# Attention products of two heads side by side in TensorE's rows, and low parts of weights on GpSimd

## The chip, the cores and the metric

One core of a Trainium2 chip runs the whole program in one launch. The metric is the device time of one execution in microseconds; lower is better. The five engines are TensorE (PE), VectorE (DVE), ScalarE (ACT), GpSimd (POOL) and SyncE (SP, which issues the DMAs). Each works through its own queue in order.

## The reference

Two blocks on a sequence of 256 rows of width 1024, in fp32. The first block runs twice a half feed-forward, a mixer and another half feed-forward. The mixer is attention in three groups (dilations 1, 4, 16) of eight heads of 64, beside a depthwise convolution of 31 taps with a layer norm:

```
q, k, v, glu_in, gates = jnp.split(h @ w_in + b_in, ...)
scores = einsum('..qhd,..khd->..hqk', qblk, kblk) / sqrt(64)   # band masks
p = exp(scores - max);  out = (p @ v) / sum(p);  softmax over the 3 groups
u = a * sigmoid(g);  u = depthwise_conv31(u) + b
y_conv = silu(layernorm(u)) @ w_proj + b_proj
y = (sigmoid(g_attn) * (attn @ w_attn_proj) + sigmoid(g_conv) * y_conv) @ w_out
```

The second block has a mixer of a recurrence and grouped attention (16 query heads, 4 key heads; three branches: compressed keys, selected blocks, window), a convolutional feed-forward, a second mixer without attention and another feed-forward:

```
y_rnn = rg_lru(conv(xr)) * gelu(gr)
o = g0 * softmax(q kc) vc + g1 * softmax(q ks) vs + g2 * softmax(q kw) vw
y = concat([y_rnn, o]) @ w_out
```

## The kernel before

Every large product is split: a weight block of 128x2048 comes from memory as `raw`, ACT casts it to `hi` (L171), DVE or POOL makes `lo = raw - hi` (L175), and three products run for each tile (L191 to L193 with the weight standing in the array, L468 to L470 with the activation standing). `raw`, `hi` and `lo` have three buffers. Where `self.share` is set, POOL makes `lo` in four pieces of 512 columns; else DVE makes it in one.

**The attention of the first block's mixer** (`head`, L656 to L698) takes one head of 64 at a time. Heads 2p and 2p+1 lie in the same tile `QK`, one in rows 0 to 63, one in rows 64 to 127, so a score product has 64 rows of contraction. Per head and half of the queries: three fp32 products into the score bank `sp` (L670), one DVE pass that adds the mask and takes the maximum (L674), exp on ACT (L677), four transposes into the bank `tp` (L680), a copy on ACT (L682), four products with `v` (L685). Each fp32 product is two passes in the trace. After four heads the sum is scaled (L693), transposed and copied (L697, L698). PSUM has one `sp` and one `tp` bank.

**The convolution** runs on DVE beside it (L614, L616). At its end POOL sums two halves (L604, `u`), PE spreads the mean (L709), DVE subtracts (L712), ACT squares (L713), POOL sums over channels (L604, `lns`), PE gives the variance (L724), ACT and PE the row of factors (L736, L738), ACT does Silu (L744), and the cast `cTh` (L492) feeds the last projection (L468).

**The attention of the second block** (`window`, L1320 to L1346, for each of two halves h of the queries, four key heads g, four repeats r) does the same with two score products per window (128 columns each for h=0, 256 for h=1), two DVE passes, two exp, and 2 or 4 transposes and products. `window_out` (L1349) gates the sum; L1377 transposes it. `compressed` and `compressed_out` handle the branch of compressed keys. The GEMM blocks of the same stage fill PE between these steps.

A list scheduler sets the order of each queue ahead of time by priority (the place in the program, shifted by `HEADS` for the first block's heads) and by when it thinks operands are there; `tc.issue_after` adds an order between two instructions and no wait.

Of the kernel before, what the change touches and what calls it, by code (L numbers as in the profile page):

```python
# [10 lines left out]
F32 = mybir.dt.float32  # L11
# [3 lines left out]
AF = mybir.ActivationFunctionType  # L15
OP = mybir.AluOpType
PSUM = bass.MemoryType.PSUM

P = 128
S = 256  # L20
# [24 lines left out]
class Net:  # L45
# [450 lines left out]
    def mixer(self, l, d, xt):  # L496
# [9 lines left out]
        with ExitStack() as es:  # L506
# [148 lines left out]
            def head(h, hd):  # L655
                self.n += 1  # L656
                if hd % 4 == 0:
# [4 lines left out]
                pr, e = hd // 2, slice((hd % 2) * 64, (hd % 2) * 64 + 64)  # L662
                sc = self.spt("sp")

                keys = (((0, 0), (1, 0)), ((h, 1),), ((h, 2),))
                o = 0
                for g in (1, 2, 0) if h else (0, 1, 2):
                    n = P * len(keys[g])
                    ks = slice(keys[g][0][0] * P, keys[g][0][0] * P + n)
                    nc.tensor.matmul(sc[:, o : o + n], QK[e, pr, g, hs], QK[e, pr, 3 + g, ks], start=True, stop=True)  # L670
                    o += n
                sm = wk.tile([P, 512], F32, tag="sg", name=f"sm{self.n}", bufs=2)
                mn = self.small.tile([P, 1], F32, tag="mn", name=f"mn{self.n}")
                dv.tensor_tensor_reduce(  # L674
                    sm, sc, self.mask1[:, h * S : h * S + 512], -0.125, 3.0e38, op0=OP.add, op1=OP.min, accum_out=mn
                )
                nc.scalar.activation(sm, sm, AF.Exp, scale=-1.0, bias=mn, accum_out=den[:, hd % 4 : hd % 4 + 1])  # L677
                pt = self.tpt(True).rearrange("p (k t) -> p k t", t=P)
                for j in range(4):
                    nc.tensor.transpose(pt[:, j], sm[:, j * P : j * P + P], self.ident)  # L680
                pT = wk.tile([P, 4, P], F32, tag="ta", name=f"pT{self.n}", bufs=2)
                nc.scalar.copy(pT, pt)  # L682
                for j, (hh, g) in enumerate(sum((keys[g] for g in ((1, 2, 0) if h else (0, 1, 2))), ())):
                    c0 = g * 512 + hd * 64
                    nc.tensor.matmul(  # L685
                        po[:, hd % 4], pT[:, j], vv[:, hh, c0 : c0 + 64], start=j == 0, stop=j == 3,
                        skip_group_check=True,
                    )
                if hd % 4 == 3:
# [353 lines left out]
    def mixer_ab(self, d, xs, nxt):  # L1043
# [4 lines left out]
        with ExitStack() as es:  # L1048
# [248 lines left out]
            def compressed_out(h, pc, cg):  # L1297
# [6 lines left out]
                for gp in range(2):  # L1304
                    po = self.pot()
# [6 lines left out]


            def window(h, g, r, po, den):
                hs = slice(h * P, h * P + P)
                nk = P * (h + 1)
                gp, e = g // 2, slice((g % 2) * 64, (g % 2) * 64 + 64)
                sc = self.spt("sp")
                for b in range(2):
                    nc.tensor.matmul(  # L1320
                        sc[:, b * nk : b * nk + nk], qr[e, gp * 4 + r, hs], kT[e, b, gp, :nk], start=True, stop=True
                    )
                pe_ = work([512], "pe")
                mn = self.small.tile([P, 2], F32, tag="mn2", name=f"mn2_{self.n}")
                for b in range(2):
                    bs = slice(b * nk, b * nk + nk)
                    dv.tensor_tensor_reduce(
                        pe_[:, bs], sc[:, bs], self.mask2[:, S - nk :], -0.125, 3.0e38,
                        op0=OP.add, op1=OP.min, accum_out=mn[:, b : b + 1],
                    )  # L1330
                    nc.scalar.activation(
                        pe_[:, bs], pe_[:, bs], AF.Exp, scale=-1.0, bias=mn[:, b : b + 1],
                        accum_out=den[:, r, b : b + 1],
                    )
                pt = self.tpt(True)
                for j in range(2 * nk // P):
                    nc.tensor.transpose(pt[:, j * P : j * P + P], pe_[:, j * P : j * P + P], self.ident)
                pT = work([512], "pT")
                nc.scalar.copy(pT[:, : 2 * nk], pt[:, : 2 * nk])
                for b in range(2):  # L1340
                    for kb in range(h + 1):
                        j = b * (h + 1) + kb
                        nc.tensor.matmul(
                            po[:, r, b], pT[:, j * P : j * P + P], vv[:, kb, b, g * 64 : g * 64 + 64],
                            start=kb == 0, stop=kb == h, skip_group_check=True,
                        )  # L1346

# [13 lines left out]
            def attend(h):  # L1361
                hs = slice(h * P, h * P + P)
                c = compressed(h)
                for g in range(4):
                    po = (self.pot() if g % 2 else self.spt("sq")).rearrange("p (r b e) -> p r b e", b=2, r=4)
                    den = self.small.tile([P, 4, 2], F32, tag="den2", name=f"den2_{h}{g}")
# [4 lines left out]
                    window_out(h, g, po, den)  # L1371
                    if g % 2 == 0:
                        continue
                    pt = self.tpt(True)
                    for j in range(4):
                        k = 2 * (g - 1) + j
                        nc.tensor.transpose(pt[:, j * P : j * P + P], ov[:, h, k * P : k * P + P], self.ident)  # L1377
                    ks = slice(2 * (g - 1), 2 * (g - 1) + 4)
# [16 lines left out]

            units = lambda c: [
# [137 lines left out]
```

## Time and profile before

| | |
|---|---|
| median of 3 runs | 2194.73 us (2192.69 to 2194.92) |
| the profiled execution | 2192.24 us, of which 2190.4 are the span |
| busy | PE 97%, DVE 65%, ACT 52%, POOL 25% of the span |
| mean granted TensorE clock | 0.988 |
| first block's attention and convolution | 323.6 to 439.6 and 1021.9 to 1138.0 us |
| its end, to the last projection | 439.6 to 468.5 and 1138.0 to 1166.8 us |
| second block's attention | 1546.4 to 1661 us, its stage to 1688.2 |

The program has five stages without attention, which the change leaves alone. A row of a profile has a time of one execution on the chip; "x6" means six instructions in a row, and a bracket behind it says how long the engine stood idle before it and what ended that.

### The profile page before, as it was taken

The numbers are of one execution on the slowest core, as the hardware profiler recorded it, in microseconds if no ns is written. First come the engines' busy times: TensorE is split into PE (matmuls) and PEld (weight loads), VectorE is DVE, ScalarE is ACT, GpSimd is POOL, SyncE is SP. The second block draws the span as 40 slices with busy tenths as digits, with TensorE's granted clock in tenths as the row PEclk, the third lists the DMA queues.
The fourth block names the chain that finished last, engine by engine and source line by source line (L and its number), as shares of the span: only waits on it lengthen the run. The fifth ranks groups of instructions, "written<-read, shape, count | busy, mean of one in ns | idle before, by whom it ended". The sixth has DMA issues, their size and how long they took to land.

```text
span 2190.4 us, 30888 instructions
## 1 busy us (share of the span) xinstructions
PE 2132.5 (97%) x12158; PEld 1826.5 (83%) x12158; DVE 1430.9 (65%) x2351; ACT 1143.3 (52%) x1582; POOL 537.4 (25%) x431
## 2 busy tenths in 40 slices
PE   8999999999999999999999999899999999999998
PEld 6887988888887788788888888678877998797997
DVE  6844788857876745398866784574555665566664
ACT  5435545565443544555565543584765554546452
POOL 3002985532001100588651200230002000203000
PEclk9999999999999999999999999998999999999999
DMA  9865563447988645455434886554323546554553
GB/s 349 315 203 170 183 192 122 140 135 269 346 294 292 196 155 202 160 191 192 138 103 156 317 290 192 167 143 149 105 77 106 183 154 211 164 186 162 182 175 113
DMA packets 233153, 415.05 MB, mean 189 GB/s; under 512 B 16048, under 2 KB 74288, under 8 KB 233008
## 3 DMA queue, kind: packets, MB, share of 16 engines
q1 hardware_dynamic: 232208, 410.99, 56.2%
q10 hardware_dynamic: 800, 2.10, 0.3%
q8 instruction: 95, 1.56, 0.3%
q14 instruction: 50, 0.41, 0.1%
HBM read 410.94 MB, written 2.11 MB: 189 GB/s over the span
## 4 chain that ended last, share of the span: by engine, by line
PE 87%; DVE 6%; ACT 3%; DMA 2%; issue 1%; POOL 1%; SPq 0%; DVEq 0%; ACTq 0%; POOLq 0%
PE mm L191 18%; PE mm L193 18%; PE mm L192 18%; PE mm L468 8%; PE mm L470 8%; PE mm L469 8%; PE sp L670 2%; PE sp L1320 1%; PE po L685 1%; PE tp L421 1%; PE sp L1192 1%; DMA mraw<-in_mod_w 1%; PE tp L680 1%; DVE lo L175 1%; DMA raw<-in_ffn_w_down 1%
## 5 line engine op out<-in xcount | busy, mean ns | idle before, releaser
L171 ACT CAST hi<-raw 128x2048 fp32r<-128x2048 f32 (+2 forms) x435 | 638.2, 1479 | 526.8 <-PE mm L193 310.5
L175 POOL TENSOR_TENSOR lo<-raw,hi 128x512 fp32r<-128x512 f32 x384 | 501.4, 1340 | 1387.8 <-ACT hi L171 1099.0
L175 DVE TENSOR_TENSOR lo<-raw,hi 128x2048 fp32r<-128x2048 f32 (+1 forms) x249 | 532.6, 2140 | 334.4 <-ACT hi L171 331.6
L191 PE MATMUL mm<-hi,xh 128*128 128x512 f32 (+1 forms) x1200 | 462.3, 386 | 8.3 <-DVE xh L278 5.6
L193 PE MATMUL mm<-hi,xl 128*128 128x512 f32 (+1 forms) x1200 | 460.6, 384 | 2.1 <-DVE xl L270 2.1
L192 PE MATMUL mm<-lo,xh 128*128 128x512 f32 (+1 forms) x1200 | 460.2, 384 | 0.8 <-POOL lo L175 0.6
L468 PE MATMUL mm<-xh,hi 128*128 128x256 f32 x1248 | 355.7, 285 | 0.9 <-ACT gc L756 0.4
L470 PE MATMUL mm<-xh,lo 128*128 128x256 f32 x1248 | 354.8, 284 | 0.0
L469 PE MATMUL mm<-xl,hi 128*128 128x256 f32 x1248 | 354.5, 284 | 0.0
L191 PEld LDWEIGHTS mm<-hi,xh 128*128 128x128 f32 x1200 | 228.1, 190 | 53.7 <-DVE xh L278 8.0
L193 PEld LDWEIGHTS mm<-hi,xl 128*128 128x128 f32 x1200 | 227.6, 190 | 46.5 <-DVE xl L270 3.8
L192 PEld LDWEIGHTS mm<-lo,xh 128*128 128x128 f32 x1200 | 228.0, 190 | 44.2 <-POOL lo L175 2.8
L468 PEld LDWEIGHTS mm<-xh,hi 128*128 128x128 f32 x1248 | 239.0, 192 | 2.7 <-ACT gc L756 0.8
L470 PEld LDWEIGHTS mm<-xh,lo 128*128 128x128 f32 x1248 | 239.0, 191 | 2.5 <-issue 1.3
L469 PEld LDWEIGHTS mm<-xl,hi 128*128 128x128 f32 x1248 | 239.1, 192 | 2.4 <-issue 1.3
L616 DVE SCALAR_TENSOR_TENSOR sp<-u,cols,sp 128x256 f32<-128x256 f32 x464 | 225.4, 486 | 7.8
L191 PE MATMUL mm<-hi,hh 128*128 128x512 f32 x528 | 210.0, 398 | 0.0
L193 PE MATMUL mm<-hi,hl 128*128 128x512 f32 x528 | 209.3, 396 | 0.0
L192 PE MATMUL mm<-lo,hh 128*128 128x512 f32 x528 | 209.0, 396 | 0.0
L846 DVE CUSTOM_DVE_ANT_0 mraw<-mraw,cact 128x1024 f32<-128x1024 f32 x96 | 117.2, 1252 | 17.8 <-DMA mraw<-in_mod_w 15.2
L193 PEld LDWEIGHTS mm<-hi,hl 128*128 128x128 f32 x528 | 99.3, 188 | 24.2
L192 PEld LDWEIGHTS mm<-lo,hh 128*128 128x128 f32 x528 | 99.3, 188 | 23.5
(337 smaller groups left out, 2676.6 us busy)
## 6 DMA issues: line engine op xcount, KB each, us to landing
raw<-in_ffn_w_up SPq DMA_DIRECT2D x98, 1024.0 KB, 6.5
raw<-in_ffn_w_down SPq DMA_DIRECT2D x60, 1024.0 KB, 5.0
mraw<-in_mod_w SPq DMA_DIRECT2D x48, 1024.0 KB, 7.4
raw<-in_w_in SPq DMA_DIRECT2D x72, 512.0 KB, 4.6
raw<-in_w_in SPq DMA_DIRECT2D x32, 1024.0 KB, 5.2
raw<-in_ffn_w_gate SPq DMA_DIRECT2D x20, 1024.0 KB, 5.2
raw<-in_ab_w_in SPq DMA_DIRECT2D x18, 1024.0 KB, 5.1
raw<-in_sc_w_in SPq DMA_DIRECT2D x12, 1024.0 KB, 5.1
```

The costliest lines, as they stand in the source:

```text
L171: nc.scalar.copy(hi[:, c : c + hi_step], raw[:, c : c + hi_step])
L175: eng.tensor_tensor(lo[:, bs], raw[:, bs], as32(hi[:, bs]), op=OP.subtract)
L191: nc.tensor.matmul(a, xh[:, k0 + k, t], wh[:, k], start=st, stop=False)
L192: nc.tensor.matmul(a, xh[:, k0 + k, t], wl[:, k], start=False, stop=False)
L193: nc.tensor.matmul(a, xl[:, k0 + k, t], wh[:, k], start=False, stop=en)
L421: nc.tensor.transpose(pt[:, j], hv[:, j * P : j * P + P], self.ident)
L468: nc.tensor.matmul(a, wh[:, k, js], xh[:, k0 + k], start=st, stop=False, skip_group_check=True)
L469: nc.tensor.matmul(a, wh[:, k, js], xl[:, k0 + k], start=False, stop=False, skip_group_check=True)
L470: nc.tensor.matmul(a, wl[:, k, js], xh[:, k0 + k], start=False, stop=en, skip_group_check=True)
L616: dv.scalar_tensor_tensor(cv[:, ch] if j == CW - 1 else acc[:, e], src, w, acc[:, e], op0=OP.mult, op1=OP.add)
L670: nc.tensor.matmul(sc[:, o : o + n], QK[e, pr, g, hs], QK[e, pr, 3 + g, ks], start=True, stop=True)
L846: dv.tensor_tensor_reduce(r, r, self.cact, 1.0, 0.0, op0=OP.mult, op1=OP.add, accum_out=self.mod[i][:, 4 * b + 2 * u + j][:, None])
```

## The change

`head` becomes `two_heads`: both heads of a tile are taken together. Their products alternate, rows 64 to 127 first, each tied behind the one before by `issue_after`. The head of rows 0 to 63 uses the bank `sp` for scores and for its transposes, the head of rows 64 to 127 uses `tp` for both. `window` becomes `windows` in the same way for key heads 2gp and 2gp+1, with two output banks held at once; `compressed_out` writes to `sp` and `tp` and comes after the second pair. `share` is set during the second block's attention and the gelu blocks behind it: four weight blocks have `lo` made by POOL instead of DVE.

```
-            def head(h, hd):
+            def two_heads(h, hd0):
...
+                bank = lambda i: self.tpt(True) if i else self.spt("sp")
+                scs = [bank(i) for i in range(2)]
+                o, last = 0, None
+                for g in order:
...
+                    for i in (1, 0):
+                        e = slice(i * 64, i * 64 + 64)
+                        with tc.issue_after(last) if last else nullcontext():
+                            last = nc.tensor.matmul(
+                                scs[i][:, o : o + n], QK[e, pr, g, hs], QK[e, pr, 3 + g, ks], start=True, stop=True
+                            ).ins
...
+                for i, sm in enumerate(sms):
...
+                    pt = bank(i).rearrange("p (k t) -> p k t", t=P)
...
-                for i in range(8):
-                    tc.cur_priority = p + HEADS[0] + HEADS[1] * i
-                    head(i // 4, 4 * e + i % 4)
+                for i in range(4):
+                    tc.cur_priority = p + HEADS[0] + 2 * HEADS[1] * i
+                    two_heads(i // 2, 4 * e + i % 2 * 2)
...
-            def window(h, g, r, po, den):
+            def windows(h, gp, r, pos, dens):
...
+                    for i in (1, 0):
+                        e = slice(i * 64, i * 64 + 64)
+                        with tc.issue_after(last) if last else nullcontext():
...
-                for g in range(4):
-                    po = (self.pot() if g % 2 else self.spt("sq")).rearrange("p (r b e) -> p r b e", b=2, r=4)
...
+                for gp in range(2):
+                    pos = [t.rearrange("p (r b e) -> p r b e", b=2, r=4) for t in (self.spt("sq"), self.pot())]
...
                     for r in range(4):
-                        window(h, g, r, po, den)
-                    if g == 0:
-                        compressed_out(h, *c)
+                        windows(h, gp, r, pos, dens)
+                        if gp == 0 and r == 1:
+                            compressed_out(h, *c)
...
+            self.share = True
             attend(0)
             attend(1)
...
+            self.share = False
```

PE's queue in the first layer's mixer, before: a head's scores (`sp`, L670), GEMM products (L191 to L193), another head's transposes (`tp`, L680) and its products with `v` (`po`, L685).

```order
1637 L685 MATMUL po_2811<-vv,pT_2864 128x64 x4
1638 L191 MATMUL mm_3215<-hi_3253,xh_1163 128x512
1639 L680 MATMUL tp_2878<-ident,sm_2874 128x128 x4
1640 L670 MATMUL sp_2918<-QK_1604 128x128 x2
1641 L670 MATMUL sp_2918<-QK_1604 128x256
1642 L685 MATMUL po_2811<-vv,pT_2883 128x64 x4
```

The same queue with the change, from a pair's scores on.

```order
1676 L192 MATMUL mm_3288<-lo_3294,xh_1163 128x512
1677 L676 MATMUL tp_2900<-QK_1604 128x128
1678 L676 MATMUL sp_2899<-QK_1604 128x128
1679 L676 MATMUL tp_2900<-QK_1604 128x128
1680 L676 MATMUL sp_2899<-QK_1604 128x128
1681 L676 MATMUL tp_2900<-QK_1604 128x256
1682 L676 MATMUL sp_2899<-QK_1604 128x256
1683 L193 MATMUL mm_3288<-hi_3293,xl_1164 128x512
```

Six products stand together where three stood, and alternate between the banks. Nine GEMM products (1683 to 1691) stand between them and the pair's first transposes.

PE's queue in the second block's attention, h=1, before: scores (L1320) of one window stand between the transposes (L1337) and the products with `v` (L1343) of others.

```order
7546 L1337 MATMUL tp_13710<-ident,abw_13704 128x128 x4
7547 L191 MATMUL mm_14098<-hi_14161,yah 128x512
7548 L1320 MATMUL sp_13750<-kTab,qr 128x256 x2
7549 L1343 MATMUL sp_13659<-vvab,abw_13715 128x64 x4
7550 L1337 MATMUL tp_13730<-ident,abw_13724 128x128 x4
7551 L192 MATMUL mm_14098<-lo_14162,yah 128x512
```

With the change, the last two pairs of h=1.

```order
7707 L1342 MATMUL sp_13743<-kTab,qr 128x256
7708 L192 MATMUL mm_14239<-lo_14310,yah 128x512
7709 L193 MATMUL mm_14239<-hi_14309,yal 128x512
7710 L192 MATMUL mm_14240<-lo_14304,yah 128x512
7711 L193 MATMUL mm_14240<-hi_14303,yal 128x512
7712 L1365 MATMUL sp_13761<-ident,abw_13749 128x128 x4
7713 L1365 MATMUL tp_13772<-ident,abw_13755 128x128 x4
7714 L1371 MATMUL sp_13659<-vvab,abw_13766 128x64 x4
7715 L1371 MATMUL po_13660<-vvab,abw_13777 128x64 x4
7716 L1342 MATMUL tp_13784<-kTab,qr 128x256
7717 L1342 MATMUL sp_13783<-kTab,qr 128x256
7718 L1342 MATMUL tp_13784<-kTab,qr 128x256
```

```order
7719 L1342 MATMUL sp_13783<-kTab,qr 128x256
7720 L1365 MATMUL sp_13801<-ident,abw_13789 128x128 x4
7721 L1365 MATMUL tp_13812<-ident,abw_13795 128x128 x4
7722 L1371 MATMUL sp_13659<-vvab,abw_13806 128x64 x4
7723 L1371 MATMUL po_13660<-vvab,abw_13817 128x64 x4
7724 L1406 MATMUL tp_13837<-ident,ov 128x128 x4
```

Scores, transposes and products of one pair stand behind one another; four GEMM products stand within the first pair and none within the second, and the transposes of the gated sum (L1406) follow the last products directly.

POOL's queue at the end of the first layer's mixer, before: weight pieces `lo`, the sum of the convolution `u`, the sums `lns` of the layer norm.

```order
51 L604 TENSOR_TENSOR u_1606<-u_1606 128x256
52 L175 TENSOR_TENSOR lo_4062<-raw_4059,hi_4061 128x512 x4
53 L604 TENSOR_TENSOR lns_3995<-sq_3927 128x512
54 L604 TENSOR_TENSOR lns_3995<-lns_3995,sq_3927 128x512 x2
55 L604 TENSOR_TENSOR lns_3995<-lns_3995 128x256
56 L175 TENSOR_TENSOR lo_4138<-raw_4135,hi_4137 128x512 x4
```

With the change:

```order
52 L604 TENSOR_TENSOR u_1606<-u_1606 128x256
53 L175 TENSOR_TENSOR lo_4062<-raw_4059,hi_4061 128x512 x4
54 L175 TENSOR_TENSOR lo_4138<-raw_4135,hi_4137 128x512 x3
55 L604 TENSOR_TENSOR lns_3995<-sq_3927 128x512
56 L175 TENSOR_TENSOR lo_4138<-raw_4135,hi_4137 128x512
57 L604 TENSOR_TENSOR lns_3995<-lns_3995,sq_3927 128x512 x2
58 L604 TENSOR_TENSOR lns_3995<-lns_3995 128x256
```

Four pieces of `lo_4138` that stood behind the layer norm's sums now stand ahead of and within them.

## Rows read from the trace of the kernel before

**Rows 1.** The page: busy us of each engine, share of the span, instructions.
```profile
PE 2132.5 (97%) x12158; PEld 1826.5 (83%) x12158; DVE 1430.9 (65%) x2351; ACT 1143.3 (52%) x1582; POOL 537.4 (25%) x431
```
**Rows 2.** Stretches: length, then busy us of each engine, granted clock, DMA share, GB/s.
```profile
323.60:439.60 116.00, 115.58 (x754) 98.86 (x753) 93.78 (x220) 67.73 (x99) 67.16 (x55) 1.00 0.41 133
...
1590.00:1661.00 71.00, 71.00 (x400) 53.07 (x400) 36.07 (x111) 45.47 (x106) 0.00 (x0) 1.00 0.20 67
```
**Rows 3.** Instructions by line: the score products of the first block's attention.
```profile
L670 PE MATMUL sp<-QK 64*128 64x128 f32 x128 | 22.9, 294 | 0.0
...
L670 PE MATMUL sp<-QK 64*128 64x256 f32 x64 | 20.6, 402 | 0.0
```
**Rows 4.** Timeline of PE around one head's scores: start, duration, instruction.
```profile
342.86 0.39 PE L192 MATMUL mm<-lo,xh 128*128 128x512 f32 x1
343.09 0.39 PE L193 MATMUL mm<-hi,xl 128*128 128x512 f32 x1
343.41 1.14 PE L670 MATMUL sp<-QK 64*128 64x256 f32 x6
344.48 0.50 PE L193 MATMUL mm<-hi,xl 128*128 128x512 f32 x1
```
**Rows 5.** Timeline of PE in the recurrence's gates, 64 by 64 products.
```profile
1440.58 0.38 PE L1115 MATMUL sp<-xc,wr 64*64 64x256 f32 x1
1440.59 0.58 PE L1115 MATMUL sp<-xc,wi 64*64 64x256 f32 x2
1440.80 0.38 PE L1115 MATMUL sp<-xc,wr 64*64 64x256 f32 x1
```
**Rows 6.** Timeline of POOL at the end of the first mixer.
```profile
437.66 1.19 POOL L604 TENSOR_TENSOR u<-u,cv 128x512 f32<-128x512 f32 x1 [16.21 <-DVE cv L616]
438.92 0.64 POOL L604 TENSOR_TENSOR u<-u 128x256 f32<-128x256 f32 x1
441.84 5.52 POOL L175 TENSOR_TENSOR lo<-raw,hi 128x512 fp32r<-128x512 f32 x4 [2.29 <-ACT hi L171]
447.33 1.30 POOL L604 TENSOR_TENSOR lns<-sq 128x512 f32<-128x512 f32 x1
...
451.46 0.72 POOL L604 TENSOR_TENSOR lns<-lns 128x256 f32<-128x256 f32 x1
```
**Rows 7.** Timeline of PE there: the variance, and the last projection's first product.
```profile
452.24 0.70 PE L724 MATMUL sp<-lns,onesd 128*128 128x256 f32 x2 [0.88 <-POOL lns L604]
...
468.47 0.80 PE L468 MATMUL mm<-cTh,hi 128*128 128x256 f32 x2 [3.97 <-ACT cTh L492]
```
**Rows 8.** Stretches behind that wait (columns as in Rows 2).
```profile
468.50:473.30 4.80, 4.80 (x21) 4.58 (x22) 3.93 (x5) 3.28 (x4) 0.00 (x0) 0.50 0.12 44
473.30:480.00 6.70, 6.70 (x58) 6.70 (x58) 2.18 (x2) 1.90 (x1) 0.00 (x0) 1.00 0.50 157
```
**Rows 9.** Timeline of PE, DVE and ACT around one window of h=1.
```profile
1643.51 1.13 PE L1320 MATMUL sp<-kTab,qr 64*128 64x256 f32 x4
...
1644.56 1.10 PE L1343 MATMUL sp<-vvab,abw 128*128 128x64 f32 x8
1644.67 0.43 DVE L1327 CUSTOM_DVE_ANT_0 abw<-sp,mask 128x256 f32<-128x256 f32 x1 [2.51 <-PE sp L1320]
...
1645.20 0.51 ACT L1331 ACTIVATE abw<-abw,mn 128x256 f32<-128x256 f32 x1 [1.00 <-DVE mn L1327]
...
1645.61 0.19 ACT L1331 ACTIVATION_READ_ACCUMULATOR abw<-abw,mn 128x1 f32 x1
```
**Rows 10.** Instructions by line of DVE, 1546.4 to 1661: the gated sums.
```profile
L1359 DVE TENSOR_TENSOR ov<-ov,abt 128x256 f32<-128x256 f32 x14 | 5.9, 420 | 0.2
...
L1353 DVE TENSOR_TENSOR abt<-sp,rd 128x512 f32<-128x512 f32 x4 | 2.8, 692 | 1.9 <-PE sp L1343 1.9
```
**Rows 11.** Instructions by line: low parts on POOL and on DVE.
```profile
L175 POOL TENSOR_TENSOR lo<-raw,hi 128x512 fp32r<-128x512 f32 x384 | 501.4, 1340 | 1387.8 <-ACT hi L171 1099.0 <-DVE lo L175 173.9 <-DVE xres L818 94.1
L175 DVE TENSOR_TENSOR lo<-raw,hi 128x2048 fp32r<-128x2048 f32 x212 | 487.9, 2302 | 280.8 <-ACT hi L171 278.2 <-DMA xnat<-xres 2.2
```

More of the change, by code (lines that the diff above doesn't have):

```diff
@@ L677, in head @@
[L677 to L687, printed above, removed]
-                    )
@@ L689, in head @@
-                if hd % 4 == 3:
+                    for i in (1, 0):
[4 more added lines that the diff above has]
+                            ).ins
+                    o += n
+                sms = []
+                for i, sc in enumerate(scs):
+                    hd = hd0 + i
+                    self.n += 1
+                    sm = wk.tile([P, 512], F32, tag="sg", name=f"sm{self.n}", bufs=2)
+                    mn = self.small.tile([P, 1], F32, tag="mn", name=f"mn{self.n}")
+                    dv.tensor_tensor_reduce(
+                        sm, sc, self.mask1[:, h * S : h * S + 512], -0.125, 3.0e38, op0=OP.add, op1=OP.min, accum_out=mn
+                    )
+                    nc.scalar.activation(sm, sm, AF.Exp, scale=-1.0, bias=mn, accum_out=den[:, hd % 4 : hd % 4 + 1])
+                    sms.append(sm)
@@ new lines, in two_heads @@
+                for i, sm in enumerate(sms):
+                    hd = hd0 + i
+                    self.n += 1
+                    pt = bank(i).rearrange("p (k t) -> p k t", t=P)
+                    for j in range(4):
+                        nc.tensor.transpose(pt[:, j], sm[:, j * P : j * P + P], self.ident)
+                    pT = wk.tile([P, 4, P], F32, tag="ta", name=f"pT{self.n}", bufs=2)
+                    nc.scalar.copy(pT, pt)
+                    for j, (hh, g) in enumerate(sum((keys[g] for g in order), ())):
+                        c0 = g * 512 + hd * 64
+                        nc.tensor.matmul(
+                            po[:, hd % 4], pT[:, j], vv[:, hh, c0 : c0 + 64], start=j == 0, stop=j == 3,
+                            skip_group_check=True,
+                        )
@@ L690, in head @@
+                if hd0 % 4 == 2:
                     rd = self.small.tile([P, 4], F32, tag="rd", name=f"rd{self.n}")
@@ L1311, in compressed_out @@
                     )
-            def window(h, g, r, po, den):
+            bank = lambda i: self.tpt(True) if i else self.spt("sp")
+            def windows(h, gp, r, pos, dens):
                 hs = slice(h * P, h * P + P)
                 nk = P * (h + 1)
-                gp, e = g // 2, slice((g % 2) * 64, (g % 2) * 64 + 64)
-                sc = self.spt("sp")
+                scs = [bank(i) for i in range(2)]
+                last = None
                 for b in range(2):
[L1320 to L1345, printed above, removed]
-                        )
@@ new lines, in windows @@
+                    for i in (1, 0):
+                        e = slice(i * 64, i * 64 + 64)
+                        with tc.issue_after(last) if last else nullcontext():
+                            last = nc.tensor.matmul(
+                                scs[i][:, b * nk : b * nk + nk], qr[e, gp * 4 + r, hs], kT[e, b, gp, :nk],
+                                start=True, stop=True,
+                            ).ins
+                pes = []
+                for sc, den in zip(scs, dens):
+                    pe_ = work([512], "pe")
+                    mn = self.small.tile([P, 2], F32, tag="mn2", name=f"mn2_{self.n}")
+                    for b in range(2):
+                        bs = slice(b * nk, b * nk + nk)
+                        dv.tensor_tensor_reduce(
+                            pe_[:, bs], sc[:, bs], self.mask2[:, S - nk :], -0.125, 3.0e38,
+                            op0=OP.add, op1=OP.min, accum_out=mn[:, b : b + 1],
+                        )
+                        nc.scalar.activation(
+                            pe_[:, bs], pe_[:, bs], AF.Exp, scale=-1.0, bias=mn[:, b : b + 1],
+                            accum_out=den[:, r, b : b + 1],
+                        )
+                    pes.append(pe_)
@@ new lines, in windows @@
+                for i, pe_ in enumerate(pes):
+                    g, po = 2 * gp + i, pos[i]
+                    pt = bank(i)
+                    for j in range(2 * nk // P):
+                        nc.tensor.transpose(pt[:, j * P : j * P + P], pe_[:, j * P : j * P + P], self.ident)
+                    pT = work([512], "pT")
+                    nc.scalar.copy(pT[:, : 2 * nk], pt[:, : 2 * nk])
+                    for b in range(2):
+                        for kb in range(h + 1):
+                            j = b * (h + 1) + kb
+                            nc.tensor.matmul(
+                                po[:, r, b], pT[:, j * P : j * P + P], vv[:, kb, b, g * 64 : g * 64 + 64],
+                                start=kb == 0, stop=kb == h, skip_group_check=True,
+                            )
```

29 lines of the change are left out of this document (11 added, 18 removed).

## The prediction

> **What bounds the kernel now.** The page comes first: TensorE (PE) is busy 97% of the span, the next engine 65% [rows 1]. So time can only go where PE has less to do, or where it waits. Then the table of stretches: in the first block's attention and convolution PE is busy 115.58 of 116.00 us and DVE 93.78; in the second block's attention PE 71.00 of 71.00, DVE 36.07, POOL 0.00 [rows 2]. Waits of PE lie at the end of each mixer, on the layer norm: 0.9 us at the variance and 4.0 at the last projection [rows 7]; behind the second PE runs at the lower of its two clocks (0.50, 21 matmuls in 4.8 us) before it is back at 1.00 [rows 8]. The question is therefore how much PE work goes, and whether the chains beside it (softmax, layer norm) can follow.
>
> **What PE saves.** A score product has 64 of 128 rows and two passes. In the gates of the recurrence two 64-row products start 10 ns apart and the next one 0.22 us later [rows 5]: two run in the time of one, and a pass of 256 columns costs 0.216. A window with four such passes takes 1.05 us up to the next product [rows 9], and some 0.09 ahead of it that shows at the head of rows 4 (a GEMM product steps by 0.23, the scores start 0.32 after the last): 1.14, so 0.28 beyond 4 x 0.216 for going into 64-row products and back. Six passes, two of 256 columns and four of 128, take 1.07 + 0.09 = 1.16 [rows 4], so a pass of 128 costs (1.16 - 0.43 - 0.28) / 4 = 0.112.
> - Products, first block, both layers: 128 passes of 128 and 64 of 256 [rows 3] are 14.3 + 13.8 = 28.1 us; run in twos they save 14.0.
> - Products, second block: 64 score products are 128 passes, half of each width: 7.2 + 13.8 = 21.0, saving 10.5.
> - Stays in 64-row products, counted in PE's queue: 44 to 26 in the first block, 42 to 16 in the second. 18 and 26 times 0.28 are 5.0 and 7.3.
>
> Together 19.0 in the first block (9.5 a layer) and 17.8 in the second: 36.8 us.
> Rows 5 show two halves that differ in rows and in columns; heads that share all columns do not occur before. From below the products save nothing, 24.5 less; from above all of it. I take all, the nearest row.
> The Trainium skill, "TensorE: Matmul & The Clock Gate", section "Part 3: Packing small matmuls — row/col tiling", gives 3.07 times for four packed row tiles, 0.77 of ideal; by it two would save an estimated 17 us and not 24.5, a size within the forecast's own range. The trace so far shows the full factor for the gates.
>
> **What the first block gives back.** PE's saving brings the end of the convolution forward only as far as DVE allows: it is busy 93.78 of 116.00, so about 9 us are there to be had, and I put the end at 428.5 (before 437.6 [rows 6]). POOL's sum follows, 1.19 + 0.64, to 430.5. Then the order decides. Before, four pieces of a weight's low part stood ahead of the layer norm's sums; now eight do. POOL needs 5.52 + 5.52 for them and 4.85 for the sums (447.33 to 452.18) [rows 6]: 430.5 + 15.9 = 446.4, against 452.2 before. PE, 9 us early, is out of other work by then and waits some 6 us at the variance. From there the same steps follow, 16.2 us from the variance to the last projection [rows 7]. ACT now has the last four heads' exps and copies among them (each at least the 0.51 of a half as wide exp [rows 9], in all some 5); I put half in the way, 2.6. So the last projection comes 5.8 - 2.6 = 3.2 us earlier, not 9.5. Ends: 0, where the second weight's cast is no earlier than before and POOL stands behind it; 9.5, where the sums keep their place in time. I take 3.0 a layer, 6 us for two; the wait of 4.0 and the slow stretch behind it I leave as they are.
>
> **What the second block gives back.** Before, the next window's scores filled the time of a softmax. Now each pair uses both banks for scores and for transposes, so the next scores wait for both copies, and only GEMM products can fill. Chain of one pair at h=1: scores end to DVE 0.11; DVE to exp 0.53; then four exps in a row at 0.60 (0.41 and the read of 0.19), the last 0.51 long [rows 9]; 0.1 to the last transposes: 0.11 + 0.53 + 1.8 + 0.51 + 0.1 = 3.05. Head 0's products with v stand behind head 1's transposes in PE's queue, so PE has only head 0's transposes (4 x 0.11) in that time: 2.6 us stay bare. GEMM products within the eight pairs of h=1, at 0.23 each [rows 4]: 3.7, 3.2, 0.9, 0, 2.1, 4.1, 0.9 and 0 us. Bare remain 0, 0, 1.7, 2.6, 0.5, 0, 1.7, 2.6 = 9.1. A weight cast on ACT in two of the chains adds 1.3 and 0.7. L1406 directly behind the last products adds, twice, the gated sum of both heads: 0.1 + 0.69 + 2 x 0.42 of the second, behind some 0.6 of the first [rows 10]: 2.3 each, 4.6. At h=0 the GEMM products within a pair last 2.1 or more: 0.3 in all. Sum 16.0: of 17.8 saved, 1.8 remain. From both sides: if the scheduler's products come when operands are there, the bare time could be half (8, leaving 10 saved); if each chain is a microsecond longer (two waits on DVE instead of one), 16 pairs add 8 to 16.
> **Low parts.** Four blocks go from DVE (2.30) to POOL (4 x 1.34 = 5.36) [rows 11]. DVE has 35 of 71 us free, so its 9.2 give nothing; POOL is idle there [rows 2]. A low part is there 3.1 later; three buffers and the distance to its use hide that, uncovered it is up to 12.
> **The pair's banks in the first block.** The wait for both copies stands there too, but nine GEMM products (2.1 us) and more stand within a pair; DVE also has convolution to do. I count nothing, at worst 1 us for each of 16 pairs.
>
> **Sum.** 2192.24 - 6 - 1.8 = 2184.4 for a profiled execution. The median of before stands 2.5 above its profile (2194.73), so 2186.9 on the scale of the runs; I say 2187. The likeliest case's own range: 2180 to 2193.
>
> **Rivals.**
> - *Most of the saving lands.* The layer norm gets its sums early (POOL's pieces wait for casts in any case, and the scheduler's guess of their time is right), 7 a layer, and the bare time in the second block is 7 instead of 16: 14 + 11 = 25, so 2169.7. For it: PE at 115.58 of 116 is what ends everything. Against: POOL's queue and the order of the pairs' rows.
> - *Slower: the pairs' chains and the clock.* In the second block's h=1, PE stands bare eight times in 40 us, 1.7 to 2.6 each. Before, a wait of 4.0 was followed by 4.8 us at 0.50 [rows 7, 8], which did 2.4 us of work. If the clock falls so for 20 of the 40 us, 10 are lost on top of 16 of bare time, against 17.8: +8.2; with the layer norm at its late end, 1 a layer: +6.2, 2201. It decides once more than 15 us of the stretch run at 0.50. For it: the shared banks leave no second window to run; against: the waits are shorter than the 4.0 of before.
> The Trainium skill, "TensorEngine Tiling (Array Packing)", section "PSUM Bottleneck", says that tiling speeds up TensorE but not the evacuation of PSUM, and that the copies may become the bottleneck. It speaks for this rival; the trace so far has DVE and ACT below two thirds of those stretches.
> - *The halves do not run together.* Heads on rows 0 and 64 share all columns, unlike rows 5; then only 5.0 and 7.3 are saved. Second block: 7.3 - 16.0 = 8.7 slower; first: 2.5 a layer less the late sums, about -1 each: +6.7, 2201.
>
> **How the numbers follow.** Chances: likeliest 0.50, most lands 0.20, slower by the clock 0.18, no concurrency 0.10, the rest 0.02. What a measurement can tell from no change is about 0.2%, 4.4 us. Faster by more: 0.7 of the likeliest (its range reaches to -2), all of the first rival, a few hundredths of the others: 0.58. Within: 0.27 of the likeliest and a third of the slower ones: 0.22. Slower: two thirds of these and a rest: 0.20. The range reaches 3 below the first rival's time and 1 above the slower ones': 2167 to 2202.
>
> **What would show it.** In the changed kernel's profile: scores of a pair starting in twos, with 0.11 or 0.22 steps for two; else the third rival. The time from the end of the convolution to the variance longer than before, PE idle there by 4 to 7 us with POOL named; if not, the first rival. In 1546 to 1690: PE idle about 16 us, named ACT or DVE between L1342, L1365 and L1406; the granted clock 1.00, or 0.50 for long stretches (the second rival). The prediction is wrong if the mixers end more than 7 us earlier each, or if the second block's attention gets longer by 4.

## The result: slower, 2210.14 us

The changed kernel takes 2210.14 us in the median of 4 runs (2201.11 to 2213.16) against 2193.72 (2192.69 to 2194.92): a ratio of 1.0068, 95% interval 1.0056 to 1.008. The forecast was 2187 and its range ended at 2202. The profile after, page, busy us by engine:

```profile
PE 2130.0 (96%) x12158; PEld 1829.3 (83%) x12158; DVE 1425.7 (65%) x2347; ACT 1144.7 (52%) x1586; POOL 551.1 (25%) x447
```

PE is as busy as before [rows 1], though half-row products now share their time; the mean granted clock fell from 0.988 to 0.971. Both programs run the same 10416 passes of GEMM products, so the time at which the same one starts shows where one is ahead. The changed kernel is 0.5 us ahead at the start, 2.6 after the first mixer, 5.3 after the second, and 19.1 behind at 1726 us. Nearly all that is lost (22.7 of these 24.4 us) is lost in the second block's attention and the projection behind it. The same stretch of GEMM products, before (length, busy us of PE, PEld, DVE, ACT, POOL, granted clock, DMA share, GB/s):

```profile
1536.50:1707.10 170.60, 166.19 (x968) 131.96 (x967) 95.52 (x256) 111.32 (x258) 16.24 (x12) 1.00 0.28 95
```

and after, as a whole and in pieces:

```profile
1532.90:1726.20 193.30, 170.43 (x968) 134.85 (x967) 91.30 (x253) 106.76 (x256) 30.94 (x24) 0.88 0.25 84
```

```profile
1532.90:1609.80 76.90, 72.81 (x512) 62.76 (x510) 40.55 (x119) 49.15 (x113) 15.02 (x12) 1.00 0.33 115
1609.80:1616.70 6.90, 6.23 (x18) 3.72 (x19) 4.21 (x8) 0.82 (x2) 0.00 (x0) 0.51 0.40 128
1616.70:1630.30 13.60, 11.83 (x67) 9.18 (x68) 3.89 (x18) 10.35 (x23) 0.00 (x0) 1.00 0.03 12
1630.30:1637.00 6.70, 6.70 (x26) 5.61 (x26) 1.62 (x1) 1.72 (x5) 0.00 (x0) 0.50 0.47 159
1637.00:1650.00 13.00, 11.22 (x60) 6.65 (x58) 5.05 (x22) 5.67 (x19) 0.00 (x0) 1.00 0.00 1
1650.00:1661.00 11.00, 9.25 (x35) 6.49 (x35) 4.39 (x10) 1.27 (x4) 0.00 (x0) 0.53 0.00 0
1661.00:1684.80 23.80, 21.98 (x140) 16.83 (x138) 9.17 (x35) 16.17 (x45) 4.96 (x4) 1.00 0.21 68
1684.80:1695.00 10.20, 8.48 (x29) 6.65 (x29) 4.46 (x8) 0.85 (x2) 0.00 (x0) 0.50 0.33 103
1695.00:1701.90 6.90, 3.59 (x16) 2.59 (x14) 3.01 (x5) 5.57 (x13) 3.62 (x3) 0.99 0.00 0
1701.90:1715.50 13.60, 7.65 (x21) 5.42 (x22) 10.05 (x22) 8.40 (x25) 7.35 (x6) 0.50 0.48 154
```

From these rows the 22.7 us (193.3 - 170.6) come apart into three terms:
- Idle PE: 193.3 - 170.43 = 22.9 after, 170.6 - 166.19 = 4.4 before: +18.5.
- Work at the lower clock: the five stretches at 0.50 to 0.53 hold 38.3 us of busy PE; busy time times (1 - clock) is 18.8 us, a little high, because a GEMM product steps by 0.43 us there and by 0.23 at 1.00, not quite twice as long. Before there is none.
- What is left of busy time, 170.43 - 18.8 = 151.6 against 166.19: -14.6, the change's saving.

What PE waited for in that stretch (us in total, times, longest):

```profile
PE tp L264 <- DVE yg L350: 7.3, 2, 7.0
PE mm L191 <- ACT hi L171: 3.4, 2, 1.8
PE sp L1365 <- DVE mn L1352: 2.7, 3, 1.3
PE mm L191 <- ACT yah L492: 2.0, 3, 0.7
PE mm L191 <- DVE xh L278: 2.0, 1, 2.0
PE tp L1406 <- DVE ov L1387: 1.9, 2, 1.0
```

and in the stretch before:

```profile
PE tp L264 <- DVE yg L350: 2.8, 3, 1.1
PE mm L191 <- DVE xh L278: 0.9, 2, 0.6
PE tp L264 <- DVE hr L235: 0.7, 1, 0.7
```

The longest wait after is not in the attention but at the end of the stage: the next norm's transposes (L264), 7.0 us. Behind the last gated transposes of attention PE's queue had 91 GEMM products before and has 24 now. Those 24 need these transposes; the other 67 could run earlier, and did, among the pairs. So the end of the stage is set by the chain of the pairs, then 24 products, then the norm, and PE has nothing to cover the norm with.

Two views belong to the prediction's steps. The pair's scores do run in twos (start, duration):

```profile
1623.42 0.38 PE L1342 MATMUL tp<-kTab,qr 64*128 64x256 f32 x1
1623.43 0.38 PE L1342 MATMUL sp<-kTab,qr 64*128 64x256 f32 x1
1623.64 0.38 PE L1342 MATMUL tp<-kTab,qr 64*128 64x256 f32 x1
```

Two passes every 0.22 us, as for the gates in [rows 5]. And POOL's queue at the end of the first mixer, with PE's variance, answers to [rows 6, 7]:

```profile
427.75 1.19 POOL L604 TENSOR_TENSOR u<-u,cv 128x512 f32<-128x512 f32 x1 [11.21 <-DVE cv L616]
...
429.61 8.75 POOL L175 TENSOR_TENSOR lo<-raw,hi 128x512 fp32r<-128x512 f32 x7
438.32 1.30 POOL L604 TENSOR_TENSOR lns<-sq 128x512 f32<-128x512 f32 x1
439.58 1.26 POOL L175 TENSOR_TENSOR lo<-raw,hi 128x512 fp32r<-128x512 f32 x1
440.80 2.60 POOL L604 TENSOR_TENSOR lns<-lns,sq 128x512 f32<-128x512 f32 x2
...
444.25 1.22 PE L740 MATMUL sp<-lns,onesd 128*128 128x256 f32 x2 [4.78 <-POOL lns L604]
```

The layer norm's sums stand behind eight pieces of weights, and PE waits 4.78 us.

### The profile page after: what moved, and what is told of

It is laid out like the page before. It is cut to its first block, busy times and chain, and to the rows that moved or that the text cites. A ratio compares the mean times of both kernels' runs of the same rounds, so it can differ in the third digit from the quotient of the medians.

```text
span 2210.3 us, 30904 instructions
## 1 busy us (share of the span) xinstructions
PE 2130.0 (96%) x12158; PEld 1829.3 (83%) x12158; DVE 1425.7 (65%) x2347; ACT 1144.7 (52%) x1586; POOL 551.1 (25%) x447
## 5 line engine op out<-in xcount | busy, mean ns | idle before, releaser
L175 POOL TENSOR_TENSOR lo<-raw,hi 128x512 fp32r<-128x512 f32 x400 | 515.5, 1323 | 1393.7 <-ACT hi L171 1080.2
L175 DVE TENSOR_TENSOR lo<-raw,hi 128x2048 fp32r<-128x2048 f32 (+1 forms) x245 | 522.3, 2133 | 328.7 <-ACT hi L171 328.3
L191 PE MATMUL mm<-hi,xh 128*128 128x512 f32 (+1 forms) x1200 | 463.2, 387 | 10.4 <-DVE xh L278 6.1
L193 PE MATMUL mm<-hi,xl 128*128 128x512 f32 (+1 forms) x1200 | 462.9, 386 | 2.0 <-DVE xl L270 2.0
L191 PEld LDWEIGHTS mm<-hi,xh 128*128 128x128 f32 x1200 | 229.0, 191 | 55.1 <-DVE xh L278 8.5
L193 PEld LDWEIGHTS mm<-hi,xl 128*128 128x128 f32 x1200 | 228.5, 190 | 46.8 <-DVE xl L270 3.8
L191 PE MATMUL mm<-hi,hh 128*128 128x512 f32 x528 | 209.9, 398 | 0.0
L193 PE MATMUL mm<-hi,hl 128*128 128x512 f32 x528 | 208.9, 396 | 0.0
L862 DVE CUSTOM_DVE_ANT_0 mraw<-mraw,cact 128x1024 f32<-128x1024 f32 x96 | 117.3, 1253 | 13.3 <-DMA mraw<-in_mod_w 10.5
L193 PEld LDWEIGHTS mm<-hi,hl 128*128 128x128 f32 x528 | 99.6, 189 | 24.0
L191 PEld LDWEIGHTS mm<-hi,hh 128*128 128x128 f32 x528 | 99.5, 188 | 23.8
```

Of the source, the lines that this page charges most:

```text
L175: eng.tensor_tensor(lo[:, bs], raw[:, bs], as32(hi[:, bs]), op=OP.subtract)
L191: nc.tensor.matmul(a, xh[:, k0 + k, t], wh[:, k], start=st, stop=False)
L193: nc.tensor.matmul(a, xl[:, k0 + k, t], wh[:, k], start=False, stop=en)
L862: dv.tensor_tensor_reduce(r, r, self.cact, 1.0, 0.0, op0=OP.mult, op1=OP.add, accum_out=self.mod[i][:, 4 * b + 2 * u + j][:, None])
```

## The experiments

**Theory A.** Pairs leave PE bare for 1 to 2 us at a time where no GEMM product fills a softmax; the granted clock falls behind these waits, and work at the lower clock costs as much as the waits. **Rivals.** B: the half-row products themselves pull the clock down. C: low parts on GpSimd come too late. D: the first block's changes do it. "The changed kernel" is the one forecast; times are medians, and ratios are against before on the same chip. The kernels ran on several chips; before took 2193.3 to 2193.7 us on each, so medians are also compared with one another.

**One block at a time.** first_only: the diff's first two parts alone (`two_heads`). second_only: the rest alone.

> Pairs in the first block's attention alone; the second block as before, low parts there on VectorE. Theory A (the loss is all in the second block's stage; the first block keeps the 2.1 and 2.7 us that the two traces show): 2193.7 - 5 = 2188.5 us. Theory B (the gain of the first block is an accident of where the granted clock falls, its two falls at 326 and 1022 us cost what the pairs save): 2194, as before.

> Pairs and shared low parts in the second block alone; the first block as before. Theory A: 2193.7 + 24 = 2218 us, or 2206 to 2220 with the spread of the changed kernel; mean granted clock near 0.975. Theory B (the second block does badly only because of what the first left behind): 2194.

Measured: 2184.58 us for the first (ratio 0.9974, 0.9956 to 0.9993; runs 2180.7 to 2194.2) and 2218.82 for the second (1.0123, 1.0106 to 1.014). Theory A on both (the first block alone gives 4 us more than its 2188.5); rival D falls. In second_only the stretch is again 193.3 us long, with 22.9 us of idle PE and the same five falls of the clock, behind waits of 1.65, 1.77, 1.28, 1.28 and 7.0 us as in the changed kernel. In first_only the stretch of the second block has its old length with the first block's pairs alone:

```profile
1522.60:1693.20 170.60, 167.41 (x968) 133.27 (x967) 95.22 (x256) 111.18 (x258) 16.26 (x12) 0.99 0.27 94
```

**Low parts.** no_share is the changed kernel less the two lines that set `share` and clear it; first_share is first_only with them:

```
-            self.share = True
             attend(0)
             attend(1)
...
-            self.share = False
```

> The changed kernel with the low parts of the second block's four weight blocks made by VectorE again. Theory A (TensorE's bare waits and the clock behind them cost the time; of POOL's low parts it waited 0.5 us): within 4 us of the changed kernel, 2206 to 2214, the same falls of the clock in the second block. Theory B (a low part that comes 3.1 us later four times holds TensorE): 2198 or less.

Measured: 2216.76 (1.0107, 1.0092 to 1.0122), 6.6 us slower than the changed kernel. Rival C falls, and so does my "within 4 us": the low parts on GpSimd help the pairs.

```profile
1528.80:1732.00 203.20, 176.14 (x967) 138.14 (x966) 95.16 (x256) 109.29 (x258) 15.94 (x12) 0.83 0.24 80
```

Idle is 27.1 here (22.9 with them), and the clock 0.83, with one fall of 34 us (1632 to 1666). By the reckoning above, 26.1 us go to the lower clock, against 18.8. The same with single windows, first_share:

> Pairs in the first block alone, single windows in the second, but the low parts of its four weight blocks on GpSimd. Theory A (they matter only where a pair's chain waits for VectorE; single windows run beside one another): within 3 us of 2184.6. Theory B (low parts on GpSimd help by themselves, as the 6.6 us between the changed kernel with and without them would have it): 2178 or less.

Measured: 2188.51 (0.9971, 0.9959 to 0.9983). The ratio of first_only, 0.9974, lies within this interval; the medians differ by 3.9, just over what A allowed, with runs of first_only spread over 13.5. Theory B falls: single windows gain nothing from it.

**Unread products in the waits.** fill, and fill_all with more of the waits (fill has its counts in the loop; both have a second loop of this kind ahead of L1406):

```
+  for _ in range(FILL.get((h, gp, r, i), 0)):
+      nc.tensor.matmul(pos[1][:, r]..., self.ident, self.ident, start=True, stop=True)
   pt = bank(i)
```

> The changed kernel with products that nobody reads in the bare waits of the second half of queries: seven of the identity with itself (128 columns, 0.22 us each) into an output bank between a pair's scores and its transposes, for the last two pairs of each group of heads, and eight into the bank of the gated sum's transposes ahead of them. Theory A (the bare waits of 1.4 to 2.6 us pull the granted clock down): the falls at 1650 and 1685 us do not come, the clock is 1.00 there, and 8 to 10 us of time go, 2200 or less. Theory B (the pairs of half-row products themselves pull it down, however busy TensorE is): the falls stay and the time is as the changed kernel's or up to 4 us longer.

> The changed kernel with unread products of the identity with itself in nearly every wait of the second block's pairs: seven between scores and transposes for the last two pairs of each group at h=1, eight in the chain that holds a weight cast, eight ahead of each half of the gated sum's transposes of h=1 and eight ahead of the second half at the end of h=0 (each 0.22 us). Theory A (waits pull the clock down; 18.8 us of the stage's 22.7 are work at half clock): of the four falls at 1610, 1630, 1650 and 1685 us three or four go, 9 to 13 us less than the changed kernel: 2197 to 2201. Theory B (half-row products pull it down): 2208 to 2214.

Measured: fill 2209.83 (1.0075, 1.006 to 1.009), no gain; fill_all 2200.93 (1.0032, 1.002 to 1.0043), 9.2 less than the changed kernel. In fill the fall at 1650 us was gone. The one at 1685 came all the same (1686 to 1693), behind a wait of 2.4 us between the two halves of the gated sum's transposes, which its products did not cover, and the two falls behind the waits for a weight cast, which fill left alone, came too. In fill_all, as a whole and where the four falls had been:

```profile
1528.70:1715.50 186.80, 171.00 (x1119) 142.09 (x1118) 92.60 (x253) 106.62 (x256) 31.45 (x24) 0.96 0.26 87
...
1607.50:1616.00 8.50, 7.65 (x44) 5.73 (x44) 4.17 (x15) 3.93 (x13) 0.00 (x0) 1.00 0.39 123
1628.00:1637.00 9.00, 8.81 (x47) 5.72 (x45) 3.82 (x11) 3.13 (x10) 0.00 (x0) 1.00 0.35 117
1645.00:1661.00 16.00, 15.32 (x101) 12.62 (x99) 6.87 (x21) 7.46 (x20) 0.00 (x0) 1.00 0.08 16
1680.00:1688.50 8.50, 7.23 (x36) 5.46 (x34) 3.31 (x5) 2.82 (x7) 2.22 (x2) 1.00 0.37 123
1688.50:1697.00 8.50, 1.23 (x6) 0.80 (x6) 5.58 (x9) 7.03 (x17) 7.79 (x7) 0.62 0.23 62
```

All four falls are gone, with the same pairs of half-row products between them (the scheduler also moved some GEMM products: 8 in place of 24 are left behind the last transposes). Rival B falls for them: it was the waits. Only the fall behind the 7 us at the stage's end stays, where nothing was filled. The stretch is 6.5 us shorter, not the 15.6 of lower clock that went (18.8 to 3.2 us): the 152 unread passes take 16.2 us of PE's time and only 7.1 of them lie in what was idle time (22.9 to 15.8). In fill the same sum gives nothing: 5.7 us of lower clock and 2.3 of idle time went, for 7.7 of unread work.

The length of a wait does not decide alone. In the changed kernel PE waits 2.56 us at 1528.5 and 1.36 at 1544.4 (L1267), and the clock stays 1.00 from 1520 to 1609. What else it takes was not tried.

**Which half of the queries.** h0_pairs keeps pairs at h=0 alone, h1_pairs at h=1 alone; the other half takes single windows (low parts on GpSimd in both).

```
                c = compressed(h)
+               if h:                       # h1_pairs: if not h
+                   for g in range(4):
+                       ...window(h, g, r, po, den)   # as before
+                   return
                for gp in range(2):
```

> The changed kernel, but the second half of queries (h=1) of the second block takes one window at a time again, with the banks of before; the first half keeps its pairs, the low parts stay on GpSimd. Theory A (pairs cost where no other window and few GEMM products lie within them, at h=1, and the clock falls there): the clock stays 1.00 from 1600 to 1660 and the stage is no longer than before; 2184.6 of the kernel with pairs in the first block alone, less up to 5 for the pairs of h=0: 2180 to 2185. Theory B (the two sums held at once and the shared banks cost in either half): 2195 or more.

> The changed kernel with single windows in the second block's first half of queries (h=0) and pairs in the second half alone; low parts on GpSimd. Theory A (a pair at h=1 is too long a chain whatever lies around it): 2200 or more. Theory C (the GEMM products are what fills a pair's waits, and the pairs of h=0 used them up; here 6 to 13 of them lie within each of the last pairs): 2178 to 2192, the clock 1.00 through h=1.

Measured: 2189.03 (0.9975, 0.9962 to 0.9989) and 2192.76 (0.9986, 0.9974 to 0.9998). Against first_share they are 0.5 and 4.3 slower; both halves together cost 21.6. The two stretches, h0_pairs and then h1_pairs:

```profile
1533.50:1707.50 174.00, 163.46 (x967) 129.10 (x966) 92.75 (x253) 107.78 (x256) 31.55 (x24) 0.97 0.27 91
```

```profile
1530.90:1707.10 176.20, 161.13 (x967) 131.25 (x966) 91.48 (x253) 107.38 (x256) 30.56 (x24) 0.94 0.27 90
```

PE idles 10.5 and 15.1 us, against 22.9 with both; 9.1 of the 15.1 lie at the stage's end, as in the changed kernel. So a pair at h=1 is not too long a chain in itself (theory A of h1_pairs falls). Theory C had the mechanism, but the time came 0.8 us above its range and the clock fell once within h=1, at 1635 us behind a wait of 1.2. In h1_pairs 10 to 24 GEMM products lie between a pair's scores and its first product with `v`, and PE waits at most 0.2 us there; in the changed kernel the last two pairs of each group have 4 and 0, and PE waits 0.15 and 1.28. What fills a pair's waits is GEMM work, and pairs in both halves draw on one stock. Most of what the halves cost together and not alone is the clock: beyond first_share's stretch (5.1 us idle, 1.7 of lower clock) they add 5.4 and 10.0 us of idle time alone and 17.8 together, but 1.8 and 4.8 us of lower clock alone and 17.1 together. For h0_pairs the miss is 4 us over the upper end: 32 GEMM products are left behind the last transposes, and 5.9 us of its idle time lie at the stage's end; the clock stayed 1.00 from 1600 to 1660, as expected.

**The layer norm.** first_ln: first_only with one line moved, so that the two blocks ahead of the layer norm have their low parts on VectorE.

```
     oT = (oT[:, 0], oT[:, 1])
+    self.share = False
...
     self.flush("ln")
-    self.share = False
```

> Pairs in the first block alone, and the two weight blocks of the attention's projection have their low parts made by VectorE, so that no weight piece stands on GpSimd between the convolution's sum and the layer norm's sums. Theory A (GpSimd's queue holds the variance, 4.8 us a layer in the changed kernel's profile): TensorE's wait at the variance goes, 3 to 9 us less than the 2184.6 of that kernel: 2176 to 2182. Theory B (the next step, ACT's part or VectorE, is as late): 2183 to 2188.

Measured: 2177.2 (0.9913, 0.9885 to 0.9941), 7.4 less than first_only and 16.4 less than before: the fastest kernel here. PE's wait at the variance:

```profile
442.86 0.70 PE L740 MATMUL sp<-lns,onesd 128*128 128x256 f32 x2 [1.52 <-POOL lns L604]
```

1.52 in place of 4.78. The edits of first_ln and h0_pairs together:

> Both of these edits together: pairs in the first block and in the second block's first half, single windows in the second half, low parts of the projection's blocks on VectorE. Theory A on both counts: 2171 to 2180. If only one holds: 2180 to 2186.

Measured: 2186.35 (0.996, 0.9946 to 0.9974): it missed the range. That is 9.2 more than first_ln, where h0_pairs stood 0.5 above first_share. Two things differ from first_ln, the pairs at h=0 and the low parts on GpSimd, and the second alone went with 3.9 us more in first_share. So pairs at h=0 do not pay either; why they cost more in this company was not tried.

**What running at once is worth.** serial: first_ln with one head's three products ahead of the other's.

```
-                for g in order:
...
-                    for i in (1, 0):
+                for i in (1, 0):
+                    o = 0
+                    for g in order:
```

> Pairs in the first block alone with low parts of the projection on VectorE (2177.2), but the products of a pair in another order: all of one head's, then all of the other's, still tied. What is lost is only that two run at once. If all 14.0 us of PE time that I counted for it reach the end: 2191; if VectorE's convolution or the layer norm bounds the mixers: 2177 to 2184. If running at once pulls the clock down at 326 and 1022 us, those falls go.

Measured: 2185.73 (0.9952, 0.9936 to 0.9969), 8.5 more than first_ln and between the two expectations. But the edit takes only a part of the running at once away. One pair in its trace:

```profile
362.98 0.60 PE L677 MATMUL tp<-QK 64*128 64x128 f32 x3
363.31 0.37 PE L677 MATMUL sp<-QK 64*128 64x128 f32 x1
363.41 0.27 PE L677 MATMUL tp<-QK 64*128 64x128 f32 x1
...
364.38 0.51 PE L193 MATMUL mm<-hi,xl 128*128 128x512 f32 x1
```

The second head (`sp`) stands behind all passes of the first (`tp`) in the program, and starts 0.33 us after it, ahead of the first head's fourth pass. Such a pair takes 1.40 or 1.61 us up to the next product, where heads in turn take 1.08; before, one head alone took 1.07. Over the 14 pairs whose products stand together that is 5.7 us of PE time, not 14.0. The other 2.8 us are not explained, and the runs of either kernel spread over 6 to 7 us. So this run does not tell what running at once is worth. The falls at 327 and 1023 us were there as well, 6.8 us each. They lie around the first pair of a layer, whose products stand apart between GEMM products, so they don't come from two products at once.

**Filling other waits.** warm: first_ln with unread products ahead of every norm's transposes in the program.

```
             pt = self.tpt().rearrange("p (k t) -> p k t", k=4)
+            for _ in range(6 if q == 0 else 0):
+                nc.tensor.matmul(pt[:, 0], self.ident, self.ident, start=True, stop=True)
```

> The kernel with pairs in the first block alone and low parts of the projection on VectorE (2177.2), with six unread products of the identity with itself (1.3 us) ahead of the first four transposes of each half of a normalised input, where PE waits for the norm. Theory A (waits pull the clock down and unread products keep it up): some of the falls at 700, 1395, 1675, 1872 and 1985 us, 2 to 10 us less: 2167 to 2175. Theory B (they only stand in the way, the falls stay): 2178 to 2195.

Measured: 2187.99 (0.9973, 0.9961 to 0.9984), 10.8 slower than first_ln, in the range of that run's theory B. It does not settle theory A, because most of the products did not land in the waits: the scheduler put most of the 20 groups (12 passes, 1.3 us each, 26 us in all) among GEMM products. The waits of 2.3 us for a norm at 1397 and 1881 us stayed, with a fall behind each; the wait of 3.9 us at 702 went, and the fall behind it too. The mean clock was 0.987 to 0.989 in its runs and 0.983 to 0.988 in those of first_ln.

## Why the prediction was wrong, step by step

**Half-row products in twos: right.** A step of 0.22 us for two, the full factor. The Trainium skill's 0.77 of ideal for packed tiles ("TensorE: Matmul & The Clock Gate", "Part 3: Packing small matmuls — row/col tiling") was measured for four tiles; these rows of two tiles show no loss. A pair of the first block takes 1.08 us with twelve passes, where one head took 1.07 with six. The saving of the second block was sized 17.8 and measured 14.6. For the first block the 14.0 us were too many: the queue splits the first pair of each layer by GEMM products (12 of the 26 stays), so only 14 of 16 pairs run in twos.

**First block: right in size, by luck.** The convolution's end was put at 428.5 and came at 427.7 (POOL's first row); the variance at 446.4 and came at 444.25; gains of 3.0 a layer were forecast, 2.1 and 2.7 measured. first_ln shows that the order on POOL holds time back: 7.4 us came when the pieces of weights left it. But the step from the variance to the last projection was wrong: sized 16.2 us plus 2.6, it took 24.0 us (444.25 to 468.29), with the clock at 0.50 from 442 to 456 us, where it had been 1.00. So the last projection came at 468.29 where it had come at 468.47 [rows 7], and at 1164.54 where it had come at 1166.81; counted from each layer's start, 0.5 and 2.6 us ahead, that is 0.3 later in both, not 3.2 earlier. What was gained is what I had left as it was: PE no longer waited there, and the slow stretch behind that wait [rows 8] was gone. In first_only, whose profile has no falls at 326 and 1022 us, the gains are 5.9 and 6.3 a layer.

**Bare time of a pair: right in size.** I worked out 2.6 us between scores and products with v where no GEMM product fills. The pair at 1646 us:

```profile
1646.46 0.38 PE L1342 MATMUL sp<-kTab,qr 64*128 64x256 f32 x1
1647.00 0.42 DVE L1352 CUSTOM_DVE_ANT_0 abw<-sp,mask 128x256 f32<-128x256 f32 x1 [4.82 <-PE sp L1342]
...
1647.46 0.51 ACT L1356 ACTIVATE abw<-abw,mn 128x256 f32<-128x256 f32 x1 [3.04 <-DVE mn L1352]
...
1648.12 0.93 PE L1365 MATMUL sp<-ident,abw 128*128 128x128 f32 x4 [1.28 <-DVE mn L1352]
...
1649.10 0.93 PE L1365 MATMUL tp<-ident,abw 128*128 128x128 f32 x4
...
1650.06 0.32 PE L1371 MATMUL sp<-vvab,abw 128*128 128x64 f32 x1
```

From the end of the last score pass, which began at 1646.46 and takes 0.22, to 1650.06 are 3.4 us; 8 transposes at 0.11 take 0.9 of them: 2.5. ACT's four exps a half microsecond apart set the pace. The Trainium skill ("TensorEngine Tiling (Array Packing)", "PSUM Bottleneck") warns that the copies out of PSUM may become the bottleneck. The limit does lie behind TensorE here, but it is the exps more than the copies: the two copies take 0.56 and 0.59 at the end of that chain.

**The step that failed: "Sum 16.0: of 17.8 saved, 1.8 remain", with the clock left out of the sum.** I held the clock's price as a rival with a chance of 0.18, because the waits (1.7 to 2.6) were shorter than the 4.0 behind which it had fallen before [rows 7, 8]. That reason was wrong, and the trace of before already showed it: the clock had fallen at 709, 1409 and 1887 us behind waits of 2.8, 2.3 and 2.3 us, and at 1989 behind two of 1.0 and 0.75:

```profile
1987.23 0.65 PE L264 MATMUL tp<-ident,yg 128*128 128x128 f32 x4 [1.01 <-DVE yg L350]
1988.64 0.94 PE L264 MATMUL tp<-ident,yg 128*128 128x128 f32 x4 [0.75 <-DVE hr L235]
```

```profile
1988.90:1992.30 3.40, 3.06 (x10) 2.20 (x9) 3.30 (x11) 3.21 (x10) 1.22 (x2) 0.50 0.40 98
```

With the change it fell four times behind waits of 1.3 to 1.8 us (1.65 and 1.77 for a weight cast on ACT, 1.28 twice between a pair's scores and transposes) and once in the 7.0 at the stage's end, and cost 18.8 us of the 22.7. fill_all showed the link: the waits filled, four falls went, and 9.2 us of the run's time with them. The rival had named the mechanism, and sized it at 10.

**The second miss: the end of the stage.** No term was there for it. At L264 and the products behind it PE waits 9.3 us (7.3 and 2.0) where it waited 4.4 before: about 5 of the 18.5 us of added idle time, because only 24 GEMM products were left where there had been 91. Of the other 13.6, 2.3 lie ahead of the first pair (L1267) and 11.3 among the pairs, forecast at 16.0. The two are not quite the same measure: the profile counts a product's tail as busy, so the pair at 1646 us shows 1.28 of its 2.5 as a wait. I had counted how many GEMM products lie within each pair, but not that they are taken from those that covered the next norm.

**Low parts on GpSimd "give nothing": wrong.** They are worth 6.6 us to the pairs. Why was not tried apart: VectorE then has 2.3 us less per block in front of a pair's chain, which is the likely reason, and most of the difference in the two traces is the lower clock (26.1 us against 18.8).

Not tried was a pair with banks of its own, which would let the next pair's scores start before both copies: whether the two shared banks or the order of the chain leaves PE bare stays open.

## What to carry to other kernels

Price a wait of TensorE twice: its length, and the work behind it at the lower clock, which here cost as much again (18.8 us beside 18.5). Whether the clock falls behind such a wait can be read from the trace of before: go through all of its falls and the waits ahead of them, not only the longest. When a change shortens TensorE's work but lengthens a chain, count the filler as one stock for the whole stage, down to what it must still cover at the stage's end. And look at every in-order queue that the new order passes: one line that moved weight pieces from GpSimd to VectorE gave 7.4 us, nearly as much as the first block's pairs alone (8.7).

## What the runs showed of the hardware beside that

The clock also fell where PE had not waited at all, and not in every trace. Around the first pair, whose six products the queue splits by GEMM products, the changed kernel and first_only have the same instructions in the same order. After:

```profile
326.50:333.00 6.50, 6.50 (x27) 5.67 (x26) 6.50 (x16) 0.31 (x1) 5.45 (x5) 0.50 0.64 204
```

first_only:

```profile
326.50:333.00 6.50, 6.50 (x50) 6.10 (x50) 6.50 (x16) 0.54 (x2) 5.51 (x5) 1.00 0.62 204
```

27 matmuls against 50 in the same 6.5 us. Such a fall of 6.8 us costs some 3.4. Each kernel has one trace, so that a fall comes in one execution and not in another of the same kernel is inferred; it is a likely part of the changed kernel's spread (12 us over 4 runs; before 2 over 4, with a single 2203.9 in 25 runs elsewhere). Why one trace has it stays open.

A short VectorE operation took seven times its time while a GpSimd piece ran, and ended with it (1684.41 and 1684.39): L1379, 0.17 us in its seven other instances, here 1.23. The reciprocal ahead of it (L1378) took its usual 0.20 beside a GpSimd piece.

```profile
1681.88 2.51 POOL L175 TENSOR_TENSOR lo<-raw,hi 128x512 fp32r<-128x512 f32 x2
1683.18 1.23 DVE L1379 TENSOR_TENSOR rd<-rd,sgab 128x8 f32<-128x8 f32 x1
```
